# Layer 0's first up-projection row: 512 modulation channels loaded in two parts, chunk 2 moved behind, eleven partial sums kept in SBUF

## The chip, the cores and the metric

One core of a Trainium2 chip runs the whole program in one launch. The metric is the device time of a run in microseconds (us); of several runs the median counts. All times below come from runs of the kernel before, or from one execution of it that the hardware profiler recorded.

## The reference

Two layers over 256 tokens of width 2048; layer 0 mixes tokens with a pooling mixer, layer 1 with attention. Every sub-layer is normed, scaled and shifted by a vector `mod` that is a matrix product of the conditioning vector with `w_ada`, so that no product with `w_up` can begin before some columns of `mod` are there.

```python
cond = jax.nn.silu(c)
for i in range(DEPTH):                               # 2 layers
    mod = cond @ w_ada[i] + b_ada[i]                 # (2048) @ (2048, 6*2048)
    sh1, sc1, g1, sh2, sc2, g2 = jnp.split(mod, 6, axis=-1)      # chunks 0 .. 5
    h = rmsnorm(x, norm_g[i, 0]) * (1 + sc1) + sh1
    y = pool_mixer(h, ...) if i == 0 else moba_attention(h, ...)
    x = x + g1 * y
    h = rmsnorm(x, norm_g[i, 1]) * (1 + sc2) + sh2
    u = conv(h @ w_up[i])                            # (256, 2048) @ (2048, 2*5632), causal, width 3
    val, gate = jnp.split(u, 2, axis=-1)
    x = x + g2 * ((silu(gate) * val) @ w_down[i])    # (256, 5632) @ (5632, 2048)
return rmsnorm(x, final_g)
```

Everything is float32. `pool_mixer` takes trailing means over 2, 4, 8 and 16 tokens in four groups of 512 channels, subtracts the token, and multiplies each group by a 512x512 matrix `pool_w`.

## The kernel before

Activations lie transposed: channel blocks of 128 on the partitions, 256 tokens along the free axis (`xT`, 16 blocks). Each product is exact to about float32 by three TensorE products of halves in fp32r: ScalarE copies a weight tile into `hi` (rounded), VectorE subtracts (`lo` = weight - `hi`), and `h` is kept as such a pair too; a product is hi x h_hi, hi x h_lo, lo x h_hi.

**Steps.** The large products are a list `steps`. A step is one 1 MB load (`w_load`, L959): 512 rows of the weight by 512 columns, tile `w`. `w_use` splits it in two halves (`hi`, `lo`, 128x1024 each, four buffers of each kind, so two steps) and 48 matmuls of 128x128 by 128x256 use them, two halves later (`LAG` = 2). A *group* is 512 output columns: `uv` groups are value columns, `ug` groups gate columns, four steps each. In layer 0 the first part of the up projection runs by *rows*: step 0 of the first `FIRST` = 11 groups, then step 1 of all, and so on, since a row needs only four of the sixteen channel blocks of `h`. Ten of these groups (`HOMES`) keep partial sums in SBUF, in *homes*: after row 0 ScalarE copies the two banks of sums out (128x512 each), after rows 1 to 3 VectorE adds them (`to_home`). The eleventh group runs in between. `T4` = 6 is the number of buffers of the tag that homes 4 and up and other tiles share.

**Start.** Before row 0 stands the pool mixer, and before that the vectors it needs. `w_ada`'s chunks 1, 0 and 2 (scale, shift, gate) come in *slices* of 512 columns, s = 3, 2, 1, 0, each as four 1 MB tiles `ws<chunk>_<slice>_<quarter>` (`slice_load`, L251); after slice s of the three chunks the pool group s is done (`pool_h`, `pool_sums`, `pool_less`, 32 products `pp` of 128x128 by 128x256, `pool_out` into `xT`, `squares`). A tile holds four 128-row blocks: VectorE multiplies by `cond` and adds into `accs` (128x512 each), ScalarE does the first, and the blocks listed in `PE_BLOCKS` go to TensorE as `row` matmuls. Small matmuls `mods` sum `accs` over partitions, and VectorE adds the bias (`mod`). After slice 0 come the norm (`ms`, `rrow`), 8 tiles for slice 0 of chunks 4 and 3, and the blocks 0 to 3 of `h`. Slices 1, 2, 3 of chunks 3 and 4 together (`pair`: eight tiles a slice, 16 additions of 128x1024, all but the first on VectorE) are loaded among the steps of rows 0 to 2.

**Order.** All loads go through SyncE's queue into one ring of five 1 MB buffers (`RAW`), in the order of the list `events`; event j + 5 is issued when the buffer of j is released by its last reader. Each engine then works its instructions in a fixed order. That order is made at build time by a scheduler in which an instruction's rank is its place in the program, moved forward by `tc.high_priority`: additions by `PRIO`, and the closing work hung to an event with `at` by 2 * `PRIO` from event `FAST` = 40 on. `VE_ON` and `AC_ON` name events in which VectorE and ScalarE keep program order strictly. All compute instructions show line L50 in the trace, a helper that issues them, so tiles tell them apart.

The main loop, in the kernel's own words:

```python
    for j, (load, use) in enumerate(events):
        while nl < min(len(events), j + RAW):
            tiles.append(events[nl][0]())
            nl += 1
        ...
        use(tiles[j])
        with tc.high_priority(offset=2 * PRIO if j >= FAST else 0):
            for f in later.get(j, ()):
                f()
```

Of the kernel before, what the change touches and what calls it, by code (L numbers as in the profile page):

```python
# [17 lines left out]
P = 128  # L18
# [38 lines left out]
def trunk(ctx: ExitStack, tc: tile.TileContext, x, c, norm_g, w_ada, b_ada, pool_w, pool_scale, w_qkv, w_o,  # L57
          rel_table, w_up, conv_w, conv_b, w_down, final_g, out):
    nc = tc.nc
# [9 lines left out]
    C = 512  # L69
# [172 lines left out]
    def slice_load(ch, s, q, pair):  # L242
# [10 lines left out]
        return load  # L253

    def slice_use(ch, s, q, pair):

        on_pe = PE_BLOCKS[ch if ch < 3 else 3 if s == 0 else 4]
        nk, w = (2, 2) if pair else (4, 1)

        def use(r):  # L260
            if q == 0:
                ada["n"] = ada.get("n", -1) + 1
                if ada["n"] == 0:
                    ada["acc"] = wt([P, D], "acc", 1, "accs")
# [17 lines left out]
            if nk * (q + 1) == KD:  # L282
                with tc.high_priority(offset=2 * PRIO):
                    if on_pe:
                        for j in range(w):
                            ac.activation(row[0:1, j * C:(j + 1) * C], ps[j][0:1, :], AF.Copy)
                    ps = ada["ps", ch, s] = aux(f"mods{ch}_{s}")
                    for j in range(4 * w):
# [149 lines left out]
    def group_T(src, nk, c0, rhs, done, name, home=None, each=None):  # L438
# [27 lines left out]

        def products(f, k, hi, lo):
            o = part(f)
            first = k % 4 if home else k
            for kk in range(2):  # L470
                h, w = rhs(k + kk), slice(f * P, (f + 1) * P)
                pe.matmul(o, hi[:, kk, w], h[:, 0:S], start=(first + kk == 0 and f % 2 == 0), stop=False,
                                 skip_group_check=True)
                pe.matmul(o, hi[:, kk, w], h[:, S:S2], start=False, stop=False, skip_group_check=True)
                pe.matmul(o, lo[:, kk, w], h[:, 0:S], start=False,
                                 stop=(k + kk == nk - 1 or (home is not None and first + kk == 3)),
                                 skip_group_check=True)

        def use_of(k0):
# [73 lines left out]
    PARTS = ((0, 4), (4, 8), (8, NG))  # L553
    HOMES, FIRST, LEAD = 10, 11, 3
    REST, MIX, PRE, SPARE = 1, 2, 2, 2
    QUIET, LATE, START = 7, -0.2, 61

    def ffn(l):
        led = 0
        for pi, (ga, gb) in enumerate(PARTS):  # L560
# [46 lines left out]
            if pi == 0:  # L607
# [3 lines left out]
                if l == 0 and MIX:  # L611
# [402 lines left out]

    later = {}
    for s in range(4)[::-1]:
        e0 = len(events)
        for n, e in enumerate(e for ch in (1, 0, 2) for e in slice_events(ch, s, False)):
            event(*e)
            if n == 5:  # L1020
                event(pool_load(s), lambda r: None)
        e1 = len(events)
        at(e0 + 5, lambda s=s: slice_done(1, s, False))
        at(e0 + 9, lambda s=s: slice_done(0, s, False))
        at(e0 + 9, lambda s=s: pool_h(s))
        at(e0 + 10, lambda s=s: pool_sums(s))
# [3 lines left out]
        at(e1 + 1, lambda s=s: slice_done(2, s, False))  # L1030
        at(e1 + 1, lambda s=s: pool_out(s))
        at(e1 + 2, lambda s=s: squares(s * GB, GB, s == 3))
        at(e0 + 1, {3: pool_start, 2: lambda: load_conv(0), 1: lambda: load_conv(1), 0: bias_rows}[s])

# [5 lines left out]

    at(e1 + 3, x1)
    slices = [slice_events(4, 0, False) + slice_events(3, 0, False)] + [slice_events(3, s, True) for s in range(1, 4)]
    for e in slices[0]:
        event(*e)
    at(len(events) - 3, lambda: slice_done(4, 0, False))
    i = 0
    for s in range(4):
        nxt = slices[s + 1] if s < 3 else []
        for g in range(FIRST):
            event(w_load(i), w_use(i))  # L1050
            i += 1
# [81 lines left out]
```

## Time and profile before

| | |
|---|---|
| median of 3 runs | 2073.59 us (2073.27 to 2078.25) |
| profiled execution | 2076.08 us, of it 2074.3 span (first to last instruction) |
| mean granted TensorE clock | 0.981 of full speed |
| TensorE matmuls busy | 2013.0 us, 97% of the span, 16292 of them |
| VectorE busy | 1641.4 us, 79%, 2023 instructions |
| ScalarE busy | 960.2 us, 46% |
| bytes moved | 558.78 MB, mean 269 GB/s |

The page's groups of rows are read as follows. In a view by stretches each engine has its busy time and its count of instructions in the stretch; a count of matmuls in a stretch of known length is a better measure of pace than the busy time, since a matmul that runs at the lower clock is busy as well. PEclk is the granted clock as a share of full speed. In a timeline the name of the tile written stands left of the arrow, and a bracket says how long the engine idled before and what released it. `x16` behind an instruction is a count; the time ahead is that of all of them, overlapping ones counted once. A float32 matmul of the program (`pp`, `row`, `mods`, `ms`) stands as two matmuls in the trace, an fp32r one as one.

### The profile page before, as it was taken

How to read it: one execution, taken by the hardware profiler on the slowest of the kernel's cores; microseconds unless marked ns; L12 is line 12 of the kernel's file. 1: busy time of each engine (PE TensorE's matmuls, PEld its weight loads, DVE VectorE, ACT ScalarE, POOL GpSimd, SP SyncE). 2: the span in 40 equal slices, each digit the busy share in tenths (PEclk: the TensorE clock that was granted, in tenths of full speed). 3: DMA queues.
4: the chain of work that ended last, by engine and by line, in shares of the span. 5: the costliest groups of instructions: out<-in, count | busy, mean ns of one | idle time of the engine just before them, and what ended most of it. 6: DMA issues, size and time to landing. Idle time of an engine off the chain costs nothing. (4 is left out here: it accounts for less than half of the span.)

```text
span 2074.3 us, 38497 instructions
## 1 busy us (share of the span) xinstructions
PE 2013.0 (97%) x16292; PEld 1907.9 (92%) x16292; DVE 1641.4 (79%) x2023; ACT 960.2 (46%) x1206; POOL 12.0 (1%) x64
## 2 busy tenths in 40 slices
PE   6898999999999999999999999999999999999998
PEld 2445999999999999999989889999999999999998
DVE  6887899899889999997787887879885666556666
ACT  3112534566454345444444444446543555435454
POOL 1000000000000000000000000000000000000000
PEclk8988999999999999999999999999999999999999
DMA  9998999655997989896888788678875555556551
GB/s 355 346 363 324 345 346 326 222 191 196 336 360 279 377 320 320 305 324 213 311 288 326 265 308 313 223 250 284 280 268 187 200 195 192 197 189 200 187 202 62
DMA packets 236445, 558.78 MB, mean 269 GB/s; under 512 B 9272, under 2 KB 9592, under 8 KB 221680
## 3 DMA queue, kind: packets, MB, share of 16 engines
q1 hardware_dynamic: 234800, 553.17, 75.4%
q8 instruction: 127, 2.08, 0.4%
q0 software_dynamic: 896, 2.49, 0.3%
q10 hardware_dynamic: 576, 0.67, 0.1%
q14 instruction: 46, 0.38, 0.0%
HBM read 554.17 MB, written 2.12 MB: 268 GB/s over the span
## 5 line engine op out<-in xcount | busy, mean ns | idle before, releaser
L50 DVE TENSOR_TENSOR lo<-w,hi 128x1024 fp32r<-128x1024 f32 x656 | 790.9, 1221 | 260.0 <-ACT hi L50 259.1
L50 ACT ACTIVATE hi<-w 128x1024 fp32r<-128x1024 f32 x656 | 683.2, 1059 | 630.5 <-PE d L50 185.6
L50 PE MATMUL uv<-h,hi 128*128 128x256 f32 x2816 | 485.1, 278 | 3.8 <-ACT h L50 3.8
L50 PE MATMUL d<-act,hi 128*128 128x256 f32 x2816 | 482.0, 277 | 0.6 <-ACT hi L50 0.6
L50 PE MATMUL ug<-h,hi 128*128 128x256 f32 x2816 | 481.8, 276 | 0.0
L50 PEld LDWEIGHTS uv<-h,hi 128*128 128x128 f32 x2816 | 426.6, 189 | 4.5 <-ACT h L50 4.1
L50 PEld LDWEIGHTS d<-act,hi 128*128 128x128 f32 x2816 | 424.9, 188 | 0.9 <-ACT hi L50 0.8
L50 PEld LDWEIGHTS ug<-h,hi 128*128 128x128 f32 x2816 | 424.0, 188 | 0.0
L50 PE MATMUL d<-act,lo 128*128 128x256 f32 x1408 | 387.4, 277 | 4.0 <-DVE lo L50 4.0
L50 PE MATMUL uv<-h,lo 128*128 128x256 f32 x1408 | 387.9, 277 | 0.0
L50 PE MATMUL ug<-h,lo 128*128 128x256 f32 x1408 | 386.3, 276 | 0.0
L50 PEld LDWEIGHTS d<-act,lo 128*128 128x128 f32 x1408 | 263.9, 188 | 4.8 <-DVE lo L50 4.8
L50 PEld LDWEIGHTS uv<-h,lo 128*128 128x128 f32 x1408 | 265.1, 189 | 0.0
L50 PEld LDWEIGHTS ug<-h,lo 128*128 128x128 f32 x1408 | 263.5, 188 | 0.0
L50 DVE SCALAR_TENSOR_TENSOR acc<-wa,cond,acc 128x2048 f32<-128x2048 f32 x105 | 246.3, 2346 | 6.6 <-DMA wa<-in_w_ada_dram 6.3
L50 DVE SCALAR_TENSOR_TENSOR accs<-ws,cond,accs 128x512 f32<-128x512 f32 (+1 forms) x179 | 157.4, 882 | 17.2 <-ACT accs L50 7.9
L50 PE MATMUL k<-h,hi 128*128 128x256 f32 x512 | 93.7, 285 | 1.1 <-ACT h L50 1.1
L50 PE MATMUL row<-ws,cond 128*1 128x512 f32 x152 | 81.5, 663 | 8.3 <-DMA ws<-in_w_ada_dram 8.3
L50 PE MATMUL q<-h,hi 128*128 128x256 f32 x512 | 88.7, 278 | 0.0
L50 PE MATMUL wo<-o,hi 128*128 128x256 f32 x512 | 88.3, 277 | 0.0
L50 PEld LDWEIGHTS k<-h,hi 128*128 128x128 f32 x512 | 80.1, 191 | 2.3 <-ACT h L50 1.4
L50 PE MATMUL v<-hi,h 128*128 128x512 f32 x256 | 80.1, 394 | 0.0
(157 smaller groups left out, 1753.9 us busy)
## 6 DMA issues: line engine op xcount, KB each, us to landing
w<-in_w_up_dram SPq DMA_DIRECT2D x176, 1024.0 KB, 5.1
wa<-in_w_ada_dram SPq DMA_DIRECT2D x112, 1024.0 KB, 5.8
w<-in_w_down_dram SPq DMA_DIRECT2D x88, 1024.0 KB, 5.1
ws<-in_w_ada_dram SPq DMA_DIRECT2D x56, 1024.0 KB, 7.6
w<-in_w_qkv_dram SPq DMA_DIRECT2D x48, 1024.0 KB, 6.4
ws<-in_w_ada_dram SPq DMA_DIRECT2D x48, 512.0 KB, 6.5
w<-in_w_o_dram SPq DMA_DIRECT2D x16, 1024.0 KB, 6.8
pw<-in_pool_w_dram SPq DMA_DIRECT2D x4, 1024.0 KB, 9.0
```

The costliest lines, as they stand in the source:

```text
L50: ins = call(*args, **kwargs)
```

## The change

1. **Chunk 2 behind.** Slices 3 and 2 come as before (chunks 1, 0, 2). Then come chunks 1 and 0 of slice 1, chunks 1 and 0 of slice 0, and only then chunk 2 of slice 1 and chunk 2 of slice 0. The same tiles, in another order.
2. **Rank of the pool.** `pool_h`, `pool_sums`, `pool_less` and `pool_product` go through `steady`: their rank is moved by `PRIO`, as that of the additions, in place of 2 * `PRIO`.
3. **Slice 0 of chunks 4 and 3 in two parts.** Each part is 256 columns of both chunks: four 1 MB tiles `wh<slice>_<part>_<quarter>` (`half_load`), each filled by two DMAs whose runs in memory are 1 KB, not 2 KB. After part 0, blocks 0 and 1 of `h` are made, after part 1, blocks 2 and 3. Part 1 is loaded among the first five steps.
4. **Row 0 in pairs.** The first ten groups' row-0 steps become ten steps that each take 256 rows of *two* groups (a tile `w` filled by two 512 KB DMAs). Five steps do rows 0 to 255 of the ten groups and copy the sums home; five more do rows 256 to 511 and add to the homes on VectorE (`use_two`). Groups ten and eleven follow as whole steps.
5. **Homes and groups.** `HOMES` 10 to 11, `FIRST` 11 to 12, `T4` 6 to 7.
6. **Squares of slice 0** are no longer added into `sqa` on VectorE (four additions); the `ms` matmuls sum all five tiles (ten matmuls for the two token tiles, two before).
7. Slice 1's eight tiles stand among the seven steps from the sixth on (eleven steps before); slices 2 and 3 among the first ten steps of their rows. The events in which the order is strict are counted anew (`ones_at`).

The core of the diff:

```diff
-    RAW, HB, LAG, T4, PRIO = 5, 4, 2, 6, 1000
+    RAW, HB, LAG, T4, PRIO = 5, 4, 2, 7, 1000
...
+    def half_load(s, part, q):
+        def load():
+            r = raw_tile(f"wh{s}_{part}_{q}")
+            rows = w_ada[0, q * 4 * P:(q + 1) * 4 * P, :].rearrange("(k p) d -> p k d", p=P)
+            for j in range(2):
+                c0 = (4 - j) * D + s * C + part * C // 2
+                nc.sync.dma_start(r.rearrange("p (k j c) -> p k j c", k=4, j=2)[:, :, j, :], rows[:, :, c0:c0 + C // 2])
...
+        def use_two(k0, hi, lo):
+            box["g"] = math.inf
+            box["a"] = [bank(f"{name}_{b}") for b in range(2)]
+            for f in range(4):
+                products(f, k0, hi, lo, True)
+            to_home(k0)
...
-    HOMES, FIRST, LEAD = 10, 11, 3
+    HOMES, FIRST, LEAD = 11, 12, 3
...
+                    for k0 in (0, 2):
+                        for a, b in zip(one[0:even:2], one[1:even:2]):
+                            uses = [twos[p[0].tensor.name, p[2]] for p in (a, b)]
+                            steps.append((a[0], k0, (a[2], b[2]),
+                                          lambda half, hi, lo, k0=k0, uses=uses: uses[half](k0, hi, lo)))
+                    steps.extend(one[even:])
...
+    order = [(ch, s) for s in (3, 2) for ch in (1, 0, 2)] + [(ch, s) for s in (1, 0) for ch in (1, 0)] + [(2, 1), (2, 0)]
...
-        at(e0 + 10, lambda s=s: pool_less(s))
+        steady(last[0, s] + 2, lambda s=s: pool_less(s))
         for f in range(GB):
-            at(e0 + 10 + f, lambda s=s, f=f: pool_product(s, f))
...
+            steady(last[0, s] + 2 + f, lambda s=s, f=f: pool_product(s, f))
...
-        at(e1 + 2, lambda s=s: squares(s * GB, GB, s == 3))
+        at(e + 1 if s else e, lambda s=s: squares(s * GB, GB, s == 3, s == 0))
...
+    at(ones_at - 1, lambda: (half_done(0, 0), h_blocks(0, 1, 0, 2)))
+    for g in range(HOMES // 2):
+        event(w_load(i), w_use(i))
+        i += 1
+        if second:
+            event(*second.pop(0))
     for s in range(4):
-        nxt = slices[s + 1] if s < 3 else []
-        for g in range(FIRST):
+        nxt = slices[s] if s < 3 else []
+        n = FIRST if s else FIRST - HOMES // 2
+        for g in range(n):
...
+            elif g == 0:
+                at(len(events) - 1, lambda: (half_done(0, 1), h_blocks(0, 1, 2, 2)))
+            while nxt and (n - SPARE) * (8 - len(nxt)) < 8 * (g + 1):
                 event(*nxt.pop(0))
...
+        with tc.high_priority(offset=PRIO if j >= FAST else 0):
+            while plain:
+                plain.pop(0)()
```

Three places show how the engines' fixed orders move. The first is TensorE at the last pool group (slice 0). `pp0_*` are its products, `row2_0_0` and `row4_0_0` the sums of chunk 2 and chunk 4 of slice 0, each from tiles `ws` as they land, `ms` the norm's sums, and a number at a name's end only tells buffers apart. Before:

```order
L50 MATMUL row2_0_0_893<-ws2_0_3_875,cond_94 1x512 x2
L50 MATMUL mods2_0_946<-ones_74,accs_206 128x1 x8
L50 MATMUL pp0_0_923<-pool_room_231,pw0_824 128x256
L50 MATMUL pp0_1_924<-pool_room_231,pw0_824 128x256 x2
L50 MATMUL pp0_0_923<-pool_room_231,pw0_824 128x256
L50 MATMUL pp0_1_924<-pool_room_231,pw0_824 128x256
L50 MATMUL pp0_0_923<-pool_room_231,pw0_824 128x256
L50 MATMUL pp0_1_924<-pool_room_231,pw0_824 128x256 x4
L50 MATMUL pp0_0_923<-pool_room_231,pw0_824 128x256 x5
L50 MATMUL pp0_1_924<-pool_room_231,pw0_824 128x256
L50 MATMUL row4_0_0_961<-ws4_0_0_891,cond_94 1x512
```

After:

```order
L50 MATMUL pp0_1_877<-pool_room_231,pw0_771 128x256 x3
L50 MATMUL row2_0_0_915<-ws2_0_0_844,cond_94 1x512
L50 MATMUL pp0_0_876<-pool_room_231,pw0_771 128x256 x2
L50 MATMUL mods2_0_958<-ones_74,accs_206 128x1 x4
L50 MATMUL pp0_0_876<-pool_room_231,pw0_771 128x256
L50 MATMUL ms_990<-mean_c_84,sqa12_419 128x1 x2
L50 MATMUL pp0_0_876<-pool_room_231,pw0_771 128x256 x2
L50 MATMUL row2_0_0_915<-ws2_0_1_867,cond_94 1x512
L50 MATMUL pp0_1_877<-pool_room_231,pw0_771 128x256 x2
L50 MATMUL row2_0_0_915<-ws2_0_1_867,cond_94 1x512
L50 MATMUL row2_0_0_915<-ws2_0_2_882,cond_94 1x512 x2
L50 MATMUL row2_0_0_915<-ws2_0_3_892,cond_94 1x512 x2
```

Before, the 32 `pp` products (those of several rows) stand between the last tile of chunk 2 and the first tile of chunk 4. After, sums of chunk 2 stand among the `pp` products, and all four tiles of chunk 2 come behind most of them.

The second place is TensorE at the sums of slice 1 (`mods3_1`), on which the next four blocks of `h` depend. `w7`, `w11`, `w12` are steps, `hi7_1` the second half of step 7. Before:

```order
L50 MATMUL ug0_3_1_1586<-h0_1_1029,hi7_1_1513 128x256 x2
L50 MATMUL ug0_3_1_1586<-h0_1_1029,lo7_1_1514 128x256
L50 MATMUL ug0_3_1_1586<-h0_1_1029,hi7_1_1513 128x256 x2
L50 MATMUL ug0_3_1_1586<-h0_1_1029,lo7_1_1514 128x256
L50 MATMUL ug0_3_1_1586<-h0_1_1029,hi7_0_1505 128x256
L50 MATMUL mods3_1_1569<-ones_74,accs_206 128x1 x8
L50 MATMUL ug0_3_1_1586<-h0_1_1029,hi7_0_1505 128x256
L50 MATMUL ug0_3_1_1586<-h0_1_1029,lo7_0_1506 128x256
```

After:

```order
L50 MATMUL ug0_5_1_1903<-h0_1_1017,hi11_1_1844 128x256 x2
L50 MATMUL ug0_5_1_1903<-h0_1_1017,lo11_1_1845 128x256
L50 MATMUL ug0_5_1_1903<-h0_1_1017,hi11_1_1844 128x256 x2
L50 MATMUL ug0_5_1_1903<-h0_1_1017,lo11_1_1845 128x256
L50 MATMUL mods3_1_1758<-ones_74,accs_206 128x1 x8
L50 MATMUL uv0_0_0_1989<-h0_1_1017,hi12_0_1898 128x256
L50 MATMUL uv0_0_1_1990<-h0_1_1017,hi12_0_1898 128x256
L50 MATMUL ug0_0_0_2054<-h0_1_1017,hi13_0_1985 128x256
```

Before, `mods3_1` stands in the middle of step 7 of the eleven steps of row 0. After, it stands behind the last product of step 11, the last of the twelve, and directly ahead of the first product of row 1.

The third place is VectorE in the same row: `lo` of a step's half, additions `accs` from tiles `ws3_1_<n>` of slice 1, and additions `home<group>` (two rows for each bank pair). Before, where slice 1 ends:

```order
L50 SCALAR_TENSOR_TENSOR accs_206<-ws3_1_5_1296,cond_94,accs_206 128x1024 x2
L50 TENSOR_TENSOR lo6_0_1439<-w6_1301,hi6_0_1438 128x1024
L50 TENSOR_TENSOR lo6_1_1448<-w6_1301,hi6_1_1447 128x1024
L50 SCALAR_TENSOR_TENSOR accs_206<-ws3_1_6_1364,cond_94,accs_206 128x1024 x2
L50 TENSOR_TENSOR lo7_0_1506<-w7_1369,hi7_0_1505 128x1024
L50 TENSOR_TENSOR lo7_1_1514<-w7_1369,hi7_1_1513 128x1024
L50 SCALAR_TENSOR_TENSOR accs_206<-ws3_1_7_1431,cond_94,accs_206 128x1024 x2
L50 TENSOR_TENSOR lo8_0_1582<-w8_1436,hi8_0_1581 128x1024
L50 TENSOR_TENSOR lo8_1_1591<-w8_1436,hi8_1_1590 128x1024
L50 TENSOR_TENSOR mod_113<-mods3_1_1569,bT_189 128x4 x2
L50 SCALAR_TENSOR_TENSOR gsc_114<-mod_113,vecs_185 128x4
L50 SCALAR_TENSOR_TENSOR ht01_4_1834<-xT_100,gsc_114,rrow_1027 128x256
```

After, at step 8 and 9:

```order
L50 SCALAR_TENSOR_TENSOR accs_206<-ws3_1_4_1462,cond_94,accs_206 128x1024
L50 TENSOR_TENSOR home1_1210<-home1_1210,ug0_1_0_1579 128x512
L50 TENSOR_TENSOR lo8_0_1616<-w8_1530,hi8_0_1615 128x1024
L50 TENSOR_TENSOR home1_1210<-home1_1210,ug0_1_1_1580 128x512
L50 TENSOR_TENSOR lo8_1_1648<-w8_1530,hi8_1_1647 128x1024
L50 TENSOR_TENSOR home2_1285<-home2_1285,uv0_2_0_1619 128x512
L50 SCALAR_TENSOR_TENSOR accs_206<-ws3_1_4_1462,cond_94,accs_206 128x1024
L50 TENSOR_TENSOR home2_1285<-home2_1285,uv0_2_1_1620 128x512
L50 TENSOR_TENSOR home2_1285<-home2_1285,ug0_2_0_1651 128x512
L50 TENSOR_TENSOR home2_1285<-home2_1285,ug0_2_1_1652 128x512
L50 TENSOR_TENSOR home3_1370<-home3_1370,uv0_3_0_1693 128x512
L50 SCALAR_TENSOR_TENSOR accs_206<-ws3_1_5_1535,cond_94,accs_206 128x1024
```

After, where slice 1 ends:

```order
L50 TENSOR_TENSOR lo12_0_1899<-w12_1687,hi12_0_1898 128x1024
L50 TENSOR_TENSOR lo12_1_1932<-w12_1687,hi12_1_1931 128x1024
L50 SCALAR_TENSOR_TENSOR accs_206<-ws3_1_7_1612,cond_94,accs_206 128x1024
L50 SCALAR_TENSOR_TENSOR accs_206<-ws3_2_0_1753,cond_94,accs_206 128x1024
L50 SCALAR_TENSOR_TENSOR accs_206<-ws3_1_7_1612,cond_94,accs_206 128x1024
L50 TENSOR_TENSOR lo13_0_1986<-w13_1767,hi13_0_1985 128x1024
L50 TENSOR_TENSOR lo13_1_1992<-w13_1767,hi13_1_1991 128x1024
L50 SCALAR_TENSOR_TENSOR accs_206<-ws3_2_1_1833,cond_94,accs_206 128x1024 x2
L50 TENSOR_TENSOR mod_113<-mods3_1_1758,bT_189 128x4 x2
L50 SCALAR_TENSOR_TENSOR gsc_114<-mod_113,vecs_185 128x4
L50 SCALAR_TENSOR_TENSOR ht01_4_1962<-xT_100,gsc_114,rrow_1015 128x256
L50 SCALAR_TENSOR_TENSOR ht01_5_1965<-xT_100,gsc_114,rrow_1015 128x256
```

Before, row 0 has no home additions on VectorE and slice 1's last addition stands between `lo7_1` and `lo8_0`. After, from `lo6_1` to slice 1's last addition (`ws3_1_7`) stand 20 home additions, 11 additions to `accs` and 12 `lo`, and then both `lo13` and two additions of slice 2 ahead of `mod` of slice 1.

## Rows read from the trace of the kernel before

**Rows 1.** The page's first part: busy time of each engine over the span.

```profile
PE 2013.0 (97%) x16292; PEld 1907.9 (92%) x16292; DVE 1641.4 (79%) x2023; ACT 960.2 (46%) x1206; POOL 12.0 (1%) x64
```

**Rows 2.** By stretch: length, busy of PE, PEld, DVE, ACT, POOL; PEclk, DMA share, GB/s.

```profile
150.00:160.00 10.00, 10.00 (x51) 5.20 (x49) 7.82 (x16) 2.26 (x3) 0.00 (x0) 1.00 1.05 403
170.00:180.00 10.00, 10.00 (x37) 8.54 (x37) 4.48 (x9) 0.00 (x0) 0.00 (x0) 0.72 0.39 150
200.00:240.00 40.00, 38.42 (x318) 38.40 (x319) 35.76 (x37) 23.39 (x32) 0.00 (x0) 0.92 1.04 386
240.00:280.00 40.00, 40.00 (x356) 40.00 (x355) 34.14 (x39) 20.87 (x27) 0.00 (x0) 1.00 0.89 316
440.00:480.00 40.00, 40.00 (x356) 40.00 (x355) 40.00 (x60) 27.48 (x37) 0.00 (x0) 1.00 0.59 195
```

**Rows 3.** Waits of PE after 205 us, largest releaser: total, number, longest.

```profile
PE d L50 <- DVE lo L50: 4.0, 3, 1.9
```

**Rows 4.** Timeline (start, length, engine): loads on SyncE's queue, pool products, first product.

```profile
139.97 0.37 SPq L251 DMA_DIRECT2D ws<-in_w_ada_dram  x1
...
167.93 13.83 SPq L251 DMA_DIRECT2D ws<-in_w_ada_dram  x2
...
170.89 9.48 PE L50 MATMUL pp<-pool_room,pw 128*128 128x256 f32 x32
180.30 5.31 PE L50 MATMUL row<-ws,cond 128*1 128x512 f32 x12
...
201.58 1.10 PE L50 MATMUL uv<-h,hi 128*128 128x256 f32 x3 [2.73 <-ACT h L50]
```

**Rows 5.** Timeline from slice 0's last additions to the first blocks of h.

```profile
165.32 0.75 DVE L50 SCALAR_TENSOR_TENSOR accs<-ws,cond,accs 128x512 f32<-128x512 f32 x1
167.78 1.22 DVE L50 TENSOR_TENSOR pool_room<-pool_room 128x1024 f32<-128x1024 f32 x1
...
179.97 0.88 DVE L50 SCALAR_TENSOR_TENSOR xT<-pp,gate,xT 128x256 f32<-128x256 f32 x2 [4.80 <-PE pp L50]
182.33 1.06 ACT L50 ACTIVATE sq<-xT 128x1024 f32<-128x1024 f32 x1 [14.55 <-DVE xT L50]
...
190.16 0.61 PE L50 MATMUL ms<-mean_c,sqa 128*128 128x1 f32 x4
196.91 1.93 PE L50 MATMUL mods<-ones,accs 128*128 128x1 f32 x16
197.03 1.99 ACT L50 ACTIVATE hi<-w 128x1024 fp32r<-128x1024 f32 x2
200.45 0.87 DVE L50 SCALAR_TENSOR_TENSOR ht<-xT,gsc,rrow 128x256 f32<-128x256 f32 x2
201.02 0.91 ACT L50 ACTIVATE h<-ht,mod 128x256 fp32r<-128x256 f32 x2 [1.74 <-DVE ht L50]
```

**Rows 6.** The page's DMA issues: form, count, size, median us from issue to landing.

```profile
w<-in_w_up_dram SPq DMA_DIRECT2D x176, 1024.0 KB, 5.1
```

**Rows 7.** Timeline of VectorE in row 1, back to back.

```profile
296.82 1.28 DVE L50 SCALAR_TENSOR_TENSOR accs<-ws,cond,accs 128x1024 f32<-128x1024 f32 x1
298.01 1.28 DVE L50 TENSOR_TENSOR home<-home,ug 128x512 f32<-128x512 f32 x2
299.21 1.22 DVE L50 TENSOR_TENSOR lo<-w,hi 128x1024 fp32r<-128x1024 f32 x1
300.35 1.28 DVE L50 SCALAR_TENSOR_TENSOR accs<-ws,cond,accs 128x1024 f32<-128x1024 f32 x1
```

**Rows 8.** Timeline of VectorE where slice 1 ends in row 0.

```profile
240.73 2.60 DVE L50 SCALAR_TENSOR_TENSOR accs<-ws,cond,accs 128x1024 f32<-128x1024 f32 x2
...
251.00 0.48 DVE L50 SCALAR_TENSOR_TENSOR h<-ht,mod,h 128x256 fp32r<-128x256 f32 x1
```

**Rows 9.** By stretch, columns as in Rows 2: after a stretch with less work.

```profile
940.00:944.00 4.00, 2.72 (x9) 2.15 (x10) 2.44 (x7) 1.42 (x3) 0.00 (x0) 0.52 0.42 133
944.00:948.00 4.00, 4.00 (x24) 4.00 (x24) 3.17 (x8) 2.90 (x5) 0.00 (x0) 0.63 0.00 0
```

More of the change, by code (lines that the diff above doesn't have):

```diff
@@ L253, in slice_load, with half_events, half_done @@
         return load
+    def half_load(s, part, q):
[5 more added lines that the diff above has]
+                nc.sync.dma_start(r.rearrange("p (k j c) -> p k j c", k=4, j=2)[:, :, j, :], rows[:, :, c0:c0 + C // 2])
+            return r
+        return load
+    def half_events(s, part):
+        return [(half_load(s, part, q), slice_use(("half", part), s, q, False)) for q in range(4)]
+    def half_done(s, part):
+        ps = ada.pop(("ps", ("half", part), s))
+        for j in range(2):
+            mod_done(0, 4 - j, 4 * s + 2 * part, 2, ps[:, 2 * j:2 * j + 2])
     def slice_use(ch, s, q, pair):
-        on_pe = PE_BLOCKS[ch if ch < 3 else 3 if s == 0 else 4]
+        on_pe = PE_BLOCKS[3 if type(ch) is tuple else ch if ch < 3 else 4]
+        name = f"h{ch[1]}" if type(ch) is tuple else ch
         nk, w = (2, 2) if pair else (4, 1)
@@ L265, in use @@
                 if on_pe:
-                    ada["row"] = [bank(f"row{ch}_{s}_{j}") for j in range(w)]
+                    ada["row"] = [bank(f"row{name}_{s}_{j}") for j in range(w)]
             odd = ada["n"] % 2
@@ L286, in use @@
                             ac.activation(row[0:1, j * C:(j + 1) * C], ps[j][0:1, :], AF.Copy)
-                    ps = ada["ps", ch, s] = aux(f"mods{ch}_{s}")
+                    ps = ada["ps", ch, s] = aux(f"mods{name}_{s}")
                     for j in range(4 * w):
@@ L412, in trunk @@
     groups = [0]
+    twos = {}
     def after(i, f):
@@ L465, in to_home, with products @@
             defer(2, adds)
-        def products(f, k, hi, lo):
+        def products(f, k, hi, lo, alone=False):
             o = part(f)
-            first = k % 4 if home else k
+            first = 0 if alone else k % 4 if home else k
             for kk in range(2):
@@ L475, in products @@
                 pe.matmul(o, lo[:, kk, w], h[:, 0:S], start=False,
-                                 stop=(k + kk == nk - 1 or (home is not None and first + kk == 3)),
+                                 stop=(k + kk == nk - 1 or (home is not None and first + kk == (1 if alone else 3))),
                                  skip_group_check=True)
+        def use_two(k0, hi, lo):
[4 more added lines that the diff above has]
+            to_home(k0)
+        twos[src.tensor.name, c0] = use_two
         def use_of(k0):
@@ L619, in ffn @@
                     rows[-1] = last + more
+                if l == 0:
+                    one = rows.pop(0)
+                    even = HOMES - HOMES % 2
+                    for k0 in (0, 2):
[4 more added lines that the diff above has]
+                    steps.extend(one[even:])
                 for r in rows:
@@ L958, in load @@
             r = raw_tile(f"w{i}")
+            if type(c0) is tuple:
+                for h, c in enumerate(c0):
+                    nc.sync.dma_start(r[:, h * 2 * C:(h + 1) * 2 * C].rearrange("p (k c) -> p k c", k=2),
+                                      src[k0 * P:(k0 + 2) * P, c:c + C].rearrange("(k p) c -> p k c", p=P))
+                return r
             nc.sync.dma_start(r.rearrange("p (k c) -> p k c", k=4),
```

50 lines of the change are left out of this document (28 added, 22 removed).

## The prediction

> **What bounds the kernel now.** I read the engine totals first: TensorE is busy for 97% of the span and VectorE for 79% [rows 1]. Then the stretches: from 201.58, the first product with `w_up` [rows 4], a stretch of 40 us holds 356 matmuls, 0.1125 us each, whatever VectorE does beside it, even where it is busy for all of the 40 [rows 2]; a step of 48 is 5.4 us. After 205 us TensorE's largest group of waits adds up to 4.0 us, the longest 1.9 [rows 3]. So the time is the start of this dense run plus a fixed rest, and a change moves it by moving the start, by putting work into the run, or by tearing a hole.
>
> What sets the start is loading, then a short chain. While loads flow, 10 us move 403 GB/s, 1 MB in 2.6 us. Between 170 and 180 it is 150 GB/s [rows 2]: SyncE issues a tile at 167.93 and the next 13.5 us later [rows 4], since these loads wait for buffers that TensorE's sums release, and those stand behind the `pp` products, 9.48 us from 170.89 [rows 4]. Behind that come `xT`, squares, the norm and the first blocks of `h` [rows 5].
>
> The Trainium skill ("DMA: Bandwidth & Descriptors", "Where 436 GB/s comes from") bounds reads from HBM near 358 GB/s, 2.9 us for 1 MB as an estimate; the 403 GB/s of this trace decide. By the same page ("Why small descriptors are slow (HBM only)") each packet costs some three cycles beside its data, so the 1 KB runs of the half tiles would cost a few per cent more, an estimate of 0.5 us over four tiles. It speaks against the change, and no run here has such runs yet.
>
> **The start.** Call M the first product with `w_up`; before, M = 201.6. The load issued at 139.97 is the seventh from the end of chunk 2's, with as many tiles ahead of it in either order. With 5.1 us from issue to landing [rows 6] and 2.6 for each further tile, the last tile of chunk 2 is there at 139.97 + 5.1 + 6 x 2.6 = 160.7. VectorE then has an addition (0.75) and the pool's last pass (1.22) ahead [rows 5]; with the hand-overs TensorE begins the `pp` products at 163.4. A `pp` is two matmuls in the trace, 0.59 as they ran here (9.48 / 16), and a `row` sum 0.88 (5.31 / 6) [rows 4]; by its half as many columns a `pp` could take 0.44. I take 0.5, for the clock here read 0.72 [rows 2]. Nine `pp` stand ahead of the first sum of chunk 2, whose buffer lets the next tile go at 163.4 + 4.5 + 0.9 = 168.8. The buffer after it waits for five more `pp` (2.5), half of chunk 2's `mods` (1.0 by 1.93 for twice as many), two `ms` (0.6) [rows 5], one sum (0.9), two `pp` (1.0) and one more sum (0.9): 175.7. One more goes at 177.5; before, the loads resume at 181.4. So the hole in the loads is there again, two tiles earlier.
>
> That tile, the last of part 0, lands at 175.7 + 5.1 + 2.6 = 183.4. Its additions stand ahead of the gate and `xT` on VectorE. From there: two additions and two small ones 1.8, four `xT` 1.8, the squares 1.1, eight `ms` 2.4 (0.61 for two) [rows 5], and what I estimate at 4.6 for root, small operations, `rrow`, `ht` (0.44) and `h` (0.45) [rows 5]: 195.1. The loads say the same: two sums of the sixth tile from that of 175.7 stand ahead of the first product, 175.7 + 5.1 + 5 x 2.6 + 1.8 = 195.6. M = 195.5, a gain of 6.1.
>
> Bounds: with loads that never pause, that sixth tile is there at 160.7 + 8 x 2.6 = 181.5 and M = 183.3, a gain of 18.3; if loads come no earlier than before, nothing is gained. I take the sum, on which both chains agree. The four additions into `sqa` that go, and the eight `ms` that come, are inside it.
>
> **What moves into the dense run.** Before, all sums for slice 0 were over at M. Now those of part 1 are partly behind it: three `row` sums (2.6) and eight `mods` (1.9): +4.5. The matmuls of the rows are as many as before. Cover for this is nothing, since TensorE is dense there.
>
> **The row behind it.** VectorE gets 20 home additions in row 0 and six in rows 1 to 3. From start to start an addition to `accs` takes 1.19 us, a home addition 0.60, a `lo` 1.14 [rows 7]. Before, there was slack: from 240 on VectorE was busy for 34.14 of 40 us [rows 2], slice 1's last addition ended at 243.33 and its first `h` was written at 251 [rows 8]; row 1 begins 11 x 5.4 = 59 us after 201.6, 10 us later still. Now `lo6_1` needs a buffer that TensorE frees at the end of step 4, M + 5 x 5.4 + 4.5 + 2.7 (the clock at the start: 318 matmuls in place of 356 from 200 to 240, 4.3 us, less the 1.6 ahead of M [rows 2]), and with `hi` (1.0 [rows 5]) and `lo` it ends at M + 36.3. Behind it stand 20 home additions, 11 large ones and 12 `lo` up to slice 1's last: 12.0 + 13.1 + 13.7 = 38.8. Then both `lo13` and two additions of slice 2 stand ahead of slice 1's `mod`, 4.7, and `mod`, `gsc`, `ht` and `h` take 1.9: M + 81.7. TensorE has done twelve steps at M + 64.8 + 7.2 = M + 72.0, and there its queue holds slice 1's sums ahead of all of row 1. A hole of 9.7 us. From below: 0, if VectorE's idle time in the first five steps lets later additions catch up, which its fixed order allows only as far as buffers are free. From above: 16, if the two `lo13` wait once more for their load, 5.1 and `hi` 1.0 [rows 5, 6].
>
> After a hole the clock falls. Where work thinned at 940, the granted clock read 0.52 and 0.63 for 8 us, with 33 matmuls in place of 71 [rows 9], 11 of these by idling: 3.0 us; by the start 2.7. I take 2.7. Rows 1 to 3 ask 62 us of VectorE for 65 on TensorE, as at 440 where it is busy all of the 40 us and TensorE loses nothing [rows 2]: no cost, and 0.6 for each home addition more if that cover failed, 4 at most. A pair tile's two DMAs are the same bytes, and 0.37 us more on SyncE's queue for an issue [rows 4] whose loads wait for buffers: nothing, 4 us for ten at worst. `T4` 7 only feeds the eleventh home.
>
> Sum: -6.1 + 4.5 + 9.7 + 2.7 = +10.8 against the profiled 2076.1, 2086.9. The median lies 2.5 under the profiled execution: 2084.
>
> **The rivals.** (A) VectorE keeps up: slice 1's sums are ready with row 0, as before, and no hole opens. For it: it has kept pace at 40 of 40 us [rows 2]. Against it: 38.8 us of work behind `lo6_1` for 36 of TensorE, and the additions behind `lo13`. Then -6.1 + 4.5 and 1 for small waits, 2073: not slower. It decides if the last addition comes before M + 65. (B) Loads flow on, because the sums come off earlier than the products' row lets me think: M = 183.3, -18.3 + 4.5 + 12.4 = -1.4, 2072, and without a hole 2061. For it: sums now stand among the `pp`. Against it: nine of sixteen are ahead of the first. (C) More is lost: `lo12` or `lo13` wait for loads issued late, by a ring of five whose last reader is VectorE, 6.1 us each: 2090 to 2096. Against it: from 240 on the loads move 316 GB/s [rows 2], with room for more. (D) That the change doesn't start sooner at all: no gain, +16.9, 2090.
>
> **How the numbers follow.** A measurement of this kernel can tell some 0.3% from no change, 6.2 us: faster is under 2067.4, slower above 2079.8. My forecast, a small gain in front and a hole that costs more, has 0.47, with 2078 to 2090 as its own range. A has 0.25, B 0.12, C 0.08, D 0.08. Slower: C, D and 0.36 of the forecast, 0.52, since its hole may be half as long. Faster: B without a hole and A with an earlier start, 0.15. Same: the rest, 0.33. The range 2066 to 2091 takes in A and leaves out B's end and most of C.
>
> **What would show it.** Right: loads pausing until 175; the first `uv` product at 193 to 198; TensorE waiting 6 to 13 us some 72 us later, for `h` of slice 1; VectorE busy without a gap ahead of that; a low clock for some us behind; then 356 matmuls in each 40 us again. Wrong: no wait at row 1 (A), first product ahead of 188 (B), VectorE waiting for `hi` and that for a load ahead of slice 1's `mod` (C), holes in rows 2 to 4 that I cost at nothing.

## The result, and the profile after

The changed kernel takes 2101.54 us (2100.44 to 2102.64, 4 runs) against 2074.77: a ratio of 1.0127, with an interval of 1.0114 to 1.0139. It is slower, as forecast, but by some 26 us and not 10. The profiled execution has a span of 2100.8 against 2074.3, 26.5 more.

The engine totals hardly moved; TensorE's share fell a point [rows 1]:

```profile
PE 2023.8 (96%) x16308; PEld 1915.8 (91%) x16308; DVE 1655.5 (79%) x2048; ACT 961.8 (46%) x1208; POOL 11.9 (1%) x64
```

Where the difference has come about shows best at a fixed piece of work far behind the change: the first product of layer 1's `k`. In the view of tile `k`, which gives first and last start, the kernel before has

```profile
L50 PE MATMUL k<-h,hi x512: 276/279/579, 942.5 to 1192.0; 128*128 128x256 f32 x171
```

and the changed one

```profile
L50 PE MATMUL k<-h,hi x512: 276/276/580, 970.0 to 1219.1; 128*128 128x256 f32 x171
```

So 27.5 us are lost ahead of 970. At the last of these products the difference is 27.1, at the end of the span 26.5: nothing is lost behind. The stretches of the changed kernel (columns as in rows 2) show two places ahead of it:

```profile
160.00:180.00 20.00, 15.52 (x73) 12.53 (x72) 12.41 (x22) 3.38 (x5) 0.00 (x0) 0.83 0.44 153
180.00:200.00 20.00, 16.42 (x56) 5.79 (x54) 7.67 (x18) 1.91 (x3) 0.00 (x0) 0.95 0.86 303
200.00:220.00 20.00, 19.06 (x99) 13.92 (x99) 12.83 (x20) 10.86 (x16) 0.00 (x0) 0.71 0.59 205
220.00:240.00 20.00, 20.00 (x145) 18.17 (x144) 13.61 (x19) 13.05 (x20) 0.00 (x0) 0.91 0.96 356
260.00:280.00 20.00, 19.19 (x167) 18.80 (x166) 20.00 (x24) 7.60 (x8) 0.00 (x0) 1.00 0.79 272
280.00:300.00 20.00, 13.29 (x88) 12.71 (x87) 19.02 (x25) 6.51 (x10) 0.00 (x0) 0.75 1.02 379
300.00:320.00 20.00, 20.00 (x177) 20.00 (x176) 14.40 (x16) 7.76 (x8) 0.00 (x0) 0.99 0.70 228
```

From 160 to 180 the loads move 153 GB/s, for twice as long as the 10 us of 150 GB/s that the rows show before [rows 2], and the matmuls from 200 to 240 are 244 where they were 318 [rows 2]. From 280 to 300 there are 88, where the old pace is 178 [rows 2], and from 260 to 280 they are 167. The stretch behind, with 177, is near the old pace.

**The start.** A timeline of the changed kernel from the loads to the first product, SyncE's queue (`SPq`), TensorE, ScalarE and VectorE put together:

```profile
143.47 15.30 SPq L251 DMA_DIRECT2D ws<-in_w_ada_dram  x7
160.11 1.63 SPq L262 DMA_DIRECT2D wh<-in_w_ada_dram  x2
176.72 0.93 SPq L262 DMA_DIRECT2D wh<-in_w_ada_dram  x2
183.33 2.63 SPq L262 DMA_DIRECT2D wh<-in_w_ada_dram  x4
...
156.49 3.59 PE L50 MATMUL row<-ws,cond 128*1 128x512 f32 x8
160.01 2.43 PE L50 MATMUL pp<-pool_room,pw 128*128 128x256 f32 x10
162.27 0.60 PE L50 MATMUL xh<-ident,x 128*128 128x128 f32 x4
169.11 6.58 PE L50 MATMUL pp<-pool_room,pw 128*128 128x256 f32 x18 [4.48 <-DVE pool_room L50]
175.63 1.02 PE L50 MATMUL row<-ws,cond 128*1 128x512 f32 x2
204.55 1.86 PE L50 MATMUL modsh<-ones,accs 1*128 1x1 f32 x8 [0.94 <-ACT accs L50]
206.34 3.57 PE L50 MATMUL rowh<-wh,cond 128*1 128x512 f32 x4
209.84 1.22 PE L50 MATMUL uv<-h,hi 128*128 128x256 f32 x4
...
162.91 1.02 ACT L50 ACTIVATE pool_room<-xh,mod,gsc 128x256 f32<-128x256 f32 x2 [2.15 <-PE xh L50]
...
167.84 1.22 DVE L50 TENSOR_TENSOR pool_room<-pool_room 128x1024 f32<-128x1024 f32 x1
192.09 0.75 DVE L50 SCALAR_TENSOR_TENSOR accs<-wh,cond,accs 128x512 f32<-128x512 f32 x1 [1.44 <-DMA wh<-in_w_ada_dram]
```

Read it from the top of TensorE's lines. The transposes `xh` of the last pool group stand behind eight `row` matmuls (four sums) of chunk 2 and ten `pp` matmuls (five products) of the group before, so ScalarE's `pool_room` starts at 162.91 and VectorE's last pass at 167.84, the very time it had before (167.78 [rows 5]), although its vectors come four tiles sooner in the list of loads. The `pp` start at 169.11. Then 18 `pp` matmuls (nine products) run, 6.58 us, and only then the first sum that frees a buffer: the tile that follows the one of 160.11 goes out at 176.72, the next at 183.33. So the pause is 16.6 us. Before, it ran from 167.93 to 181.4 [rows 4], 13.5, with four more tiles of the list already issued ahead of it. Part 0's last tile is added at 192.09, and the first `w_up` product comes at 209.84, 8.3 us later than before.

**The hole.** The timelines of VectorE and TensorE at the end of row 0 (a bracket is TensorE's wait and what ended it):

```profile
282.70 3.69 DVE L50 SCALAR_TENSOR_TENSOR accs<-ws,cond,accs 128x1024 f32<-128x1024 f32 x3
286.28 2.37 DVE L50 TENSOR_TENSOR lo<-w,hi 128x1024 fp32r<-128x1024 f32 x2
288.55 2.61 DVE L50 SCALAR_TENSOR_TENSOR accs<-ws,cond,accs 128x1024 f32<-128x1024 f32 x2
291.09 0.22 DVE L50 TENSOR_TENSOR mod<-mods,bT 128x4 f32<-128x4 f32 x2
...
286.44 1.95 PE L50 MATMUL mods<-ones,accs 128*128 128x1 f32 x16 [1.54 <-DVE accs L50]
292.62 0.79 PE L50 MATMUL uv<-h,hi 128*128 128x256 f32 x2 [4.24 <-ACT h L50]
294.77 0.58 PE L50 MATMUL uv<-h,hi 128*128 128x256 f32 x1 [0.93 <-DVE h L50]
```

TensorE ends row 0 at 284.90 (286.44 less the wait of 1.54) and begins row 1 at 292.62. The sums are ready at 288.4, but VectorE works both `lo13` and two additions of slice 2 until 291.09, then `mod`. Behind it the granted clock is at half (0.50) for some 8 us:

```profile
292.00:296.00 4.00, 2.45 (x9) 2.15 (x10) 3.39 (x6) 0.91 (x2) 0.00 (x0) 0.50 1.05 408
296.00:300.00 4.00, 4.00 (x20) 4.00 (x20) 3.73 (x7) 0.91 (x2) 0.00 (x0) 0.50 1.05 406
300.00:304.00 4.00, 4.00 (x35) 4.00 (x34) 1.40 (x2) 0.00 (x0) 0.00 (x0) 0.95 1.01 337
```

**The account.** First product 209.84 - 201.58 = 8.3. Row 0 from there to 284.90 takes 75.1. In the kernel before, the same 576 products would take 64.8 at the old pace, 2.7 more by the slow first stretch, and 1.9 more for slice 1's own sums, which stood inside the row: 69.4, so 5.7 are lost. (In the changed kernel these sums lie in the hole.) Then 7.7 to row 1. From 292.62 to 304 there are 64 matmuls where 101 would fit, 4.2; 0.93 of these are the wait for `h` in the timeline, the rest is the clock. Together 25.9, of the 27.5 at `k`; the other 1.6 were not traced.

The 5.7 of row 0 are a net figure. Between 218.69 and 231.20 TensorE spends 4.5 us on part 1 (three `row` sums and both halves of `modsh`). Behind them its clock falls, and later it waits for `lo` and `hi` of a step, as two stretches show. In return the first 48 products take 6.4 us, 7.9 before.

```profile
232.00:236.00 4.00, 4.00 (x23) 4.00 (x22) 2.90 (x5) 3.44 (x6) 0.00 (x0) 0.57 0.75 289
272.00:276.00 4.00, 3.19 (x26) 2.79 (x25) 4.00 (x5) 1.61 (x2) 0.00 (x0) 1.00 1.03 391
```

### The profile page after: what moved, and what is told of

Its sections match the earlier page's. It is cut to its first block, busy times and chain, and to the rows that moved or that the text cites. A ratio compares the mean times of both kernels' runs of the same rounds, so it can differ in the third digit from the quotient of the medians.

```text
span 2100.8 us, 38600 instructions
## 1 busy us (share of the span) xinstructions
PE 2023.8 (96%) x16308; PEld 1915.8 (91%) x16308; DVE 1655.5 (79%) x2048; ACT 961.8 (46%) x1208; POOL 11.9 (1%) x64
## 5 line engine op out<-in xcount | busy, mean ns | idle before, releaser
L50 DVE SCALAR_TENSOR_TENSOR accs<-ws,cond,accs 128x512 f32<-128x512 f32 (+1 forms) x161 | 144.0, 899 | 24.2 <-ACT accs L50 10.2
L50 PEld LDWEIGHTS wo<-o,hi 128*128 128x128 f32 x512 | 77.4, 188 | 0.1
```

The lines of the kernel that those rows point to most:

```text
L50: ins = call(*args, **kwargs)
```

## The experiments

Each ratio is to the kernel before, from runs on the same chip, with its 95% interval; 0.001 is 2.07 us. "First product" is the first `uv` in the profile of one execution; how far such a figure can be trusted stands in the last section.

**The order of the chunks, the pool's rank and the squares alone.** The kernel before, with

```diff
+    order = [(ch, s) for s in (3, 2) for ch in (1, 0, 2)] + [(ch, s) for s in (1, 0) for ch in (1, 0)] + [(2, 1), (2, 0)]
...
-        at(e0 + 10, lambda s=s: pool_less(s))
+        steady(last[0, s] + 2, lambda s=s: pool_less(s))
```

> The kernel before with parts 1, 2 and 6 of the change alone (order of the chunks, rank of the pool, squares of slice 0), rows as before. Theory: the loads still pause behind the pool's products, so the first product with w_up comes at 200 to 207 and the time is 2074 to 2081. Rival (the order does start sooner, and only the halves and pairs spoil it): first product near 195, 2068.

Measured: 1.0051 (1.0032 to 1.0071), 10.6 us slower; the profiled execution 13.3. The first product came at 216.4. The stretch from 170 to 180 (columns as in rows 2):

```profile
170.00:180.00 10.00, 10.00 (x32) 6.24 (x32) 4.99 (x11) 1.06 (x1) 0.00 (x0) 0.71 0.27 86
```

The theory said "no gain" and the run said "a loss", more than either expectation: fewer loads come in the pause, 86 GB/s against 150 [rows 2]. The rival, that order alone starts sooner, is out.

**The other half: the start as before.** The changed kernel with

```diff
+    order = [(ch, s) for s in (3, 2, 1, 0) for ch in (1, 0, 2)]
...
     def steady(i, f):
-        at(i, lambda: plain.append(f))
+        at(i, f)
```

> The changed kernel with the order of the chunks and the pool's rank as before; halves, pairs and eleven homes stay. Theory: the start's share goes in part, the hole behind row 0 and the sums moved into the dense run stay: first product at 202 to 207, a wait of 6 to 9 us at row 1, 2091 to 2098. Rival (the start does not matter): as the changed kernel, 2101.

Measured: 1.007 (1.005 to 1.009), 14.5 us slower than before, somewhat less than the theory's range. First product 194.4 in this execution; three later kernels with the same order of the chunks and rank had 199.4, 200.9 and 201.7. The two halves of the change thus cost 10.6 and 14.5, and add up to 25.1 of the 26.3 that 1.0127 makes. Each of the two is uncertain by some 4 us, and the squares (part 6) are in both, so this is no more than consistent.

**VectorE in program order at row 1.** `VE_ON` also names four events, from the one ahead of row 1's first step on:

```diff
-    PE_ON, VE_ON, AC_ON = (), (ones_at - 1, ones_at, ones_at + 1), (...)
+    PE_ON, VE_ON, AC_ON = (), (ones_at - 1, ones_at, ones_at + 1) + tuple(range(row1 - 1, row1 + 3)), (...)
```

> The changed kernel, VectorE kept to program order over the first four events of row 1, so that slice 1's mod comes ahead of the two lo13 and two additions of slice 2. Theory: the hole is VectorE's, and shrinks by 4.8 us less some 2 us for the sums' round trip over TensorE: 2097 to 2099. Rival (the hole is not VectorE's order but loads): 2101 or more.

Measured: 1.0104 (1.0089 to 1.012), 4.8 us less than the whole change; the two intervals just touch. TensorE's timeline at row 1:

```profile
284.74 2.25 PE L50 MATMUL mods<-ones,accs 128*128 128x1 f32 x16 [0.52 <-DVE accs L50]
288.57 0.80 PE L50 MATMUL uv<-h,hi 128*128 128x256 f32 x2 [1.58 <-ACT h L50]
```

From 284.22 to 288.57 are 4.35 us in place of 7.72, and `k` starts 3.4 us sooner, at 966.6. This share of the hole is VectorE's order, as the prediction had it.

**No load behind the pool's products.** The changed kernel, with

```diff
-        on_pe = PE_BLOCKS[3 if type(ch) is tuple else ch if ch < 3 else 4]
+        on_pe = () if (ch, s) in ((2, 0), (("half", 0), 0)) else PE_BLOCKS[3 if type(ch) is tuple else ch if ch < 3 else 4]
```

> The changed kernel, with chunk 2 of slice 0 and part 0 of chunks 4 and 3 summed on VectorE alone, so that no load waits for sums that stand behind the pool's products on TensorE. Theory: loads flow on from 160, the first product comes 8 to 14 us sooner (196 to 202), 2088 to 2094. Rival (the pool's chain or VectorE's additions set the start, not the loads): first product at 206 or later, 2098 to 2102.

Measured: 1.0084 (1.0069 to 1.0099), 8.9 us less. First product 199.5. The stretches from 160 to 180 move 382 and 282 GB/s:

```profile
160.00:170.00 10.00, 5.52 (x33) 4.82 (x33) 9.78 (x16) 2.33 (x4) 0.00 (x0) 0.90 1.07 382
170.00:180.00 10.00, 9.55 (x36) 7.73 (x34) 10.00 (x19) 1.06 (x1) 0.00 (x0) 0.76 0.83 282
```

With the order of chunks and the pool as in the change (its products begin at 169.31), and only the sums taken off TensorE, the start's loss is gone. So neither the pool nor VectorE made it. The edit does two things at once: no load waits for these sums, and TensorE does not spend time on them. That the loads did wait is shown by the stretches; how much of the gain is the second was not separated.

**Order or rank?** The changed kernel with the pool at its old rank:

```diff
     def steady(i, f):
-        at(i, lambda: plain.append(f))
+        at(i, f)
```

> The changed kernel with the pool's rank as before (2 * PRIO), the new order of the chunks kept. Theory: it is the new order of the chunks that delays the start (the pool's transposes stand behind sums of chunk 2 on TensorE, and chunk 2's sums then behind all 16 pool products): first product at 208 to 214, 2099 to 2105. Rival (the lower rank delays the pool): first product at 195 to 202, 2087 to 2094.

Measured: 1.011 (1.0093 to 1.0126), first product 208.6. Some 3 us less than the whole change, with overlapping intervals: the order of the chunks, with the squares, carries the loss, the rank little of it or none. The opposite pairing, new rank and old order, was not tried.

**Without row 0's home additions.** The sums of rows 256 to 511 for the first ten groups are left out:

```diff
                 products(f, k0, hi, lo, True)
-            to_home(k0)
+            if k0 == 0:
+                to_home(k0)
```

> The changed kernel without the 20 home additions of row 0 on VectorE: the sums over rows 256 to 511 of the first ten groups are left out, all else is as in the changed kernel. Theory: VectorE has 12 us less ahead of slice 1's mod, the hole at row 1 (6.7 us of waits, 3.2 by the clock behind it) closes: 2090 to 2093. Rival (the hole is set by loads of slice 1 or by the fixed order, not by VectorE's work): 2097 to 2102.

Measured: 1.0063 (1.0043 to 1.0082), 13.2 us less. No hole is left:

```profile
280.00:300.00 20.00, 20.00 (x179) 20.00 (x178) 18.41 (x22) 10.58 (x13) 0.00 (x0) 1.00 0.88 297
```

The hole and what follows it are 7.7 + 4.2 = 11.9 in the changed kernel. In this profile `k` starts at 959.1, 10.9 us sooner, although the first product came 1.9 later (211.8). VectorE's 20 additions are enough to make the hole.

**Four groups in pairs.** The start as before, halves and eleven homes, but

```diff
-                    even = HOMES - HOMES % 2
+                    even = 4
```

with part 1's four loads among the first two steps.

> The start of the kernel before (order of the chunks and rank), halves and eleven homes as in the change, but only the first four groups in pairs: 8 home additions in row 0 and not 20. Theory: the start gain of 7 us of the run before stays, VectorE ends slice 1 in time, the hole goes, and what is left are the sums in the dense run: 2072 to 2079. Rival (it is not VectorE's additions but the later sums and loads that cost): 2084 to 2089.

Measured: 1.0067 (1.0047 to 1.0087), as with ten groups in pairs: a miss. No wait is left at the end of row 0, but another has come near its start, ahead of part 1's blocks of `h`, and 220 to 240 holds 125 matmuls at a clock of 0.77:

```profile
221.37 0.80 PE L50 MATMUL uv<-h,hi 128*128 128x256 f32 x2 [2.79 <-ACT h L50]
```

```profile
220.00:240.00 20.00, 17.70 (x125) 17.41 (x126) 17.89 (x23) 5.18 (x7) 0.00 (x0) 0.77 0.94 353
```

The pairs are what covers the loading and the sums of part 1. Fewer pairs move the hole from the end of row 0 to its start.

**The kernel before, chunk 4 on VectorE.**

```diff
-        on_pe = PE_BLOCKS[ch if ch < 3 else 3 if s == 0 else 4]
+        on_pe = () if (ch, s) == (4, 0) else PE_BLOCKS[ch if ch < 3 else 3 if s == 0 else 4]
```

> The kernel before, with chunk 4 of slice 0 summed on VectorE alone, nothing else changed: no load waits for sums behind the pool's products on TensorE. Theory: the pause of 13.5 us in the loads goes, the first product comes at 192 to 197 in place of 201.6: 2065 to 2070. Rival (VectorE's six more additions, 4.4 us, or the chain behind the pool take it back): 2073 to 2077.

Measured: 1.0004 (0.9994 to 1.0014), no change; the rival was right. The pause goes (396 GB/s from 170 to 180 against 150 [rows 2]), yet the first product comes only 2.5 us sooner, at 199.1, and `k` starts at 942.4 as before. In the two profiles the 2.5 us are nearly gone after 48 products (209.34 against 209.47): TensorE waits 1.20 for `h` behind its first four, and its clock, at 0.50 from 200 to 204 in both, then comes back later.

```profile
201.49 0.58 PE L50 MATMUL uv<-h,hi 128*128 128x256 f32 x1 [1.20 <-DVE h L50]
204.00:208.00 4.00, 4.00 (x23) 4.00 (x23) 3.44 (x3) 0.45 (x1) 0.00 (x0) 0.58 0.65 195
```

In the kernel before:

```profile
204.00:208.00 4.00, 4.00 (x27) 4.00 (x27) 3.96 (x6) 1.66 (x3) 0.00 (x0) 0.71 1.04 358
```

Since 2.5 us is less than one profile can place a start by, the time ratio is the firm finding here, and this account of it is not.

**Chunk 2 wholly off TensorE.** The changed kernel, with `(2, 1)`, `(2, 0)` and part 0 summed on VectorE.

```diff
+        on_pe = () if (ch, s) in ((2, 1), (2, 0), (("half", 0), 0)) else PE_BLOCKS[...]
```

> The changed kernel with chunk 2 of slices 1 and 0 and part 0 summed on VectorE alone, so that neither the transposes of the last pool group nor the loads stand behind sums of chunk 2 on TensorE. Theory (the pool waits in TensorE's fixed order behind chunk 2's sums): its products begin 5 to 9 us sooner than the 169.1 of the changed kernel, the loads do not pause, first product at 195 to 200, 2087 to 2092. Rival (the pool's chain is set by its vectors or by VectorE): products at 168 or later, no gain over the run that spared slice 0 alone, 2092 to 2097.

Measured: 1.0089 (1.0074 to 1.0104). The pool's products begin at 162.70, 6.4 us sooner:

```profile
162.70 9.27 PE L50 MATMUL pp<-pool_room,pw 128*128 128x256 f32 x32 [2.48 <-DVE pool_room L50]
```

So chunk 2's sums did hold the pool up, as the theory has it. The first product, at 198.4, and the time are no better than without slice 1's share (199.5 and 1.0084), as the rival had it: the earlier pool gains nothing here. TensorE now waits 12.0 us in three waits for VectorE's sums, 7.3 in the longest, which follows the pool's products: there VectorE's pace takes the place of TensorE's queue.

**Ten homes, eleven groups.**

```diff
-    RAW, HB, LAG, T4, PRIO = 5, 4, 2, 7, 1000
+    RAW, HB, LAG, T4, PRIO = 5, 4, 2, 6, 1000
...
-    HOMES, FIRST, LEAD = 11, 12, 3
+    HOMES, FIRST, LEAD = 10, 11, 3
```

> The changed kernel with ten homes and eleven groups in a row, and six buffers of the shared tag, as before. Theory: part 5 of the change costs little, since row 0 loses as much work on TensorE as on VectorE and the hole stays: 2099 to 2103. Rival (the eleventh home's additions or the larger row make the hole): 2090 to 2096.

Measured: 1.0163 (1.0148 to 1.0178), 7.5 us slower than the whole change, outside both expectations. Of this 2.1 us stand at the first product already (211.9), in this execution. The wait for slice 1's sums grew from 1.5 to 3.8:

```profile
286.17 3.57 PE L50 MATMUL mods<-ones,accs 128*128 128x1 f32 x16 [3.79 <-DVE accs L50]
293.98 0.80 PE L50 MATMUL uv<-h,hi 128*128 128x256 f32 x2 [4.23 <-ACT h L50]
```

and 280 to 300 holds 66 matmuls, not 88. Row 1 begins 82.1 us after the first product, where it was 82.8 in the changed kernel and 83.9 with the old start: it follows VectorE's work and not TensorE's. The twelfth group is a step of 5.4 us of TensorE's work ahead of the hole and only 2.3 of VectorE's, so without it the hole is longer, 11.6 (from 282.38) in place of 7.7. Part 5 of the change covers the others' cost. `T4` went with it and was not separated.

**Six groups in pairs**, with the start as before (`even = 6`, part 1's loads among three steps).

> The start of the kernel before, halves and eleven homes, six groups in pairs: 12 home additions in row 0. A middle between ten groups (hole at row 1) and four (hole ahead of part 1's blocks of h). Theory: both holes shrink, and with the start of 195 to 201 it comes to 2080 to 2086. Rival (each early start is paid back whole, since the same tiles must be loaded and summed before the second half of h): 2087 to 2092.

Measured: 1.0054 (1.0038 to 1.0071), 11.2 us slower than before, inside the first expectation. Both holes shrink, 155 matmuls from 220 to 240 and 170 from 260 to 280, but neither is gone. Of the kernels with halves that compute everything it has the lowest ratio, and it is still slower than before.

**Both savings.** The start as before, and VectorE in program order at row 1.

> The start of the kernel before, halves, pairs and eleven homes as in the change, and VectorE in program order at row 1. Theory: the two savings add up, 15.4 us by the start and 4.2 by the order, from 2101.5 to 2082 to 2087. Rival (with an earlier start VectorE is later against TensorE and the hole grows back): 2088 to 2092.

Measured: 1.0069 (1.0054 to 1.0084). No gain over the start alone (1.007) is seen, in the range of the rival. But the hole did not grow back, as the rival had it:

```profile
275.92 2.04 PE L50 MATMUL mods<-ones,accs 128*128 128x1 f32 x16 [0.29 <-DVE accs L50]
279.54 0.79 PE L50 MATMUL uv<-h,hi 128*128 128x256 f32 x2 [1.58 <-ACT h L50]
```

It is 3.9 us (from 275.63), against 9.3 with the old start alone, whose row 1 is

```profile
270.59 2.78 PE L50 MATMUL mods<-ones,accs 128*128 128x1 f32 x16 [1.56 <-DVE accs L50]
278.30 0.79 PE L50 MATMUL uv<-h,hi 128*128 128x256 f32 x2 [4.93 <-ACT h L50]
```

In these two executions the first product came 6.5 us later here (200.9 and 194.4), and `k` starts at nearly the same time (958.1 and 958.7). The intervals are too wide to rule out the 4 us, so whether the two add up in time is open.

## Why the prediction was wrong

**The bound** (dense products; the time is the start, holes and work moved into the dense run) held as a way to account for the loss: with the clock behind a hole, these make 25.9 of 27.5. It does not say that an earlier start is kept: the run of the kernel before with chunk 4 on VectorE started 2.5 sooner in its profile and took the same time.

**The start failed**, and it is most of the miss. Predicted: first product at 195.5, a gain of 6.1. Measured: 209.84, a loss of 8.3, so 14.3 us off. The step that failed is "with the hand-overs TensorE begins the `pp` products at 163.4". I counted from the last tile of chunk 2 and VectorE's last pass, and did not follow that pass back through ScalarE's `pool_room` to the transposes on TensorE, which stand behind chunk 2's sums of slice 1. The `pp` began at 169.11, 5.7 late. (The time of 139.97 from which I counted did not hold either: the seventh tile from the end of chunk 2's, the first line of the timeline above, goes out at 143.47 in the changed kernel, 3.5 later.) Then a `pp` took 0.73 (6.58 / 9) and not 0.5, 2.1 more. With that the second buffer came at 183.3 and not 175.7, and part 0's last tile at 192.1 and not 183.4. The chain behind that tile was reckoned at 12 and took 17.7. Up to the end of `ms` it ran nearly as reckoned (6.8 us, 192.1 to 198.9, for 7.1); the 4.6 estimated from the root to `h` became 10.9, because on TensorE a sum of part 1 (1.87), both halves of `modsh` (1.71 and 1.86) and two more sums of part 1 (3.57, about twice the 1.88 that four such matmuls took at 225.26, where the clock was at full) stand between `ms` and the first product. What the runs put in place of it: the new order leaves four tiles of chunk 2 and one of part 0 in the five buffers when the pool starts, where before it was tiles four places further on, so the loads stop sooner, and the pool itself starts no earlier. Order, rank and squares on the kernel before cost 10.6, and the rank has little part in it; taking the sums off TensorE gives 8.9 back.

Rival (D), no gain at the start, was nearest in its mechanism, with a chance of 0.08, and even it did not go below nothing; (C) reached further in time, to 2096, by waits for loads at row 1 that did not come. The bounds said "if loads come no earlier than before, nothing is gained"; a loss was not among them, for no stated reason.

**Work moved into the dense run**: predicted 4.5, and TensorE spends 4.5 on these sums. Right. Row 0 as a whole loses 5.7, by the clock behind the sums and by short waits, which the prediction put at nothing.

**The hole**: predicted from M + 72.0 to M + 81.7. Measured from M + 75.1 to M + 82.8, 7.7 in place of 9.7, with the two `lo13` and two additions ahead of `mod` where the order had them. The run in program order and the one without home additions bear out both halves of the reason. Right in mechanism and in where it ends; it is shorter by the three microseconds that TensorE lost earlier in the row. The sum of the prediction counts all 9.7 as new, although 1.9 of them are slice 1's own sums, which stood in the row before.

**The clock** behind it: predicted 2.7, measured 4.2, of it 0.93 a wait for `h`. **Rows 1 to 3**: nothing predicted, and from 304 to 560 the counts are 177 to 179 in 20 us. **Part 5**: the prediction gave it no share of its own (of `T4` it says "only feeds the eleventh home"); with part 5 undone it got 7.5 worse, so it is a cover that the prediction did not see.

The terms other than the start sum to 16.9 predicted and 17.6 measured. That the sums agree so well is in part luck, since the hole is 2.0 shorter and the row and the clock 1.2 and 1.5 longer. The weighed rule on short runs ("DMA: Bandwidth & Descriptors", "Why small descriptors are slow (HBM only)", in the Trainium skill) shows no loss that matters here: while half tiles and steps came in by turns, 12 us moved 392 GB/s, against 403 with 2 KB runs alone [rows 2]:

```profile
192.00:204.00 12.00, 8.89 (x34) 5.27 (x34) 4.01 (x13) 1.67 (x4) 0.00 (x0) 0.75 1.06 392
```

## What to carry to other kernels

A load that waits for a buffer waits for everything that stands ahead of the buffer's last reader on that reader's engine; when loads are put in another order, ask which tiles sit in the ring when the long piece of work begins, and follow that work's own inputs back over every engine before giving it an earlier time. An earlier start is worth only what the engines can keep up behind it: here halves with few pairs starve TensorE at the start of the row, and with many pairs VectorE at its end. And a bound needs its other side: "no gain" is not the worst case of a reordering.

## What the runs showed of the hardware

The kernel with the old start and the one that adds VectorE's program order at row 1 have the same TensorE instructions in the same order up to the first product. Their profiles have it at 194.4 and 200.9. The second was 2.2 us behind at about 150 already, and its pool products took longer, with a granted clock of 0.66 from 170 to 180 where the first had 1.00:

```profile
170.99 7.17 PE L50 MATMUL pp<-pool_room,pw 128*128 128x256 f32 x32
...
174.36 9.28 PE L50 MATMUL pp<-pool_room,pw 128*128 128x256 f32 x32
```

Two executions of the same work differ by 6.5 us, so one profile places a start only within some 7 us. The loss at the start is outside of that: the five kernels with the new order and the sums on TensorE that have halves had the first product at 208.6 to 211.9, the two with the sums on VectorE at 198.4 and 199.5.

A gap in TensorE's work cost more than its length: the 7.7 us of the hole were followed by 11.4 us in which 64 matmuls ran where 101 would fit, with the granted clock at 0.50 for the first 8.
